# A bidirectional state space model beside attention: chunks of 16 tokens instead of 8, scans over four channel groups at once, and coefficients and softmax scaling moved off GpSimd

## The chip, the cores and the metric

One core of a Trainium2 chip runs the whole program. The metric is the device time of one execution in microseconds; the median of several executions counts. Engines are named as in the profile: PE (TensorE), DVE (VectorE), ACT (ScalarE), POOL (GpSimd), SP (which issues the DMAs).

## The reference

One encoder layer over 2048 tokens of width 1024, in float32. A projection gives q, k, v and a state space input u of 512 channels (32 groups of 16). Windowed attention and the state space model run on the same tokens; their outputs are joined, projected and followed by a feed-forward part.

```python
h  = rms_norm(x, norm1)
z  = h @ w_in                        # q (8 heads) | k, v (2 heads) | u (512)
a  = windowed_gqa(q, k, v, q_gain, k_gain, sink)
# s5_mixer, for each group g (16 channels) and both directions, 64 complex states:
abr, abi = mag * cos(li * dt), mag * sin(li * dt)
bur, bui = u_g @ bbr.T, u_g @ bbi.T
x_t = (abr + i abi) * x_{t-1} + (bur + i bui)_t
y   = d_skip * u + sum_dir( xr @ c_re.T - xi @ c_im.T )
s   = glu(gelu(y) @ w_glu)
x   = x + concat([a, s]) @ w_out
x   = x + square(relu(rms_norm(x, norm2) @ w_ff1)) @ w_ff2
```

## The kernel before, in words

**Stages.** From 0 to 132 us x is normalised and transposed and u is computed (`u_part`); beside that, `ssm_setup` makes the small tables of the state space model on DVE. From 132 to 362 us `qkv_part` makes q, k and v, tile by tile of 128 tokens. From 362 to about 790 us the attention runs, in 32 units (a block of 128 queries, and one of two key heads): `front` has scores and `softmax`, `back` the transposes of the probabilities, their product with v and the output projection. Then come the GLU, the second norm and the two feed-forward products, which the change does not touch.

**The side stream.** The state space model itself has no stage of its own: it is a Python generator, `side_stream`, that the qkv and attention loops advance. `Side.step(cost)` adds `cost * SIDE_STEPS / SIDE_MAIN` to a counter and takes that many steps of the generator; a `yield` in its functions ends a step. After the last group the stream loads w_glu and prepares the first quarter of the GLU. The recording layer then places each engine's instructions by an estimate of its own, so that an engine's queue is near the written order, but not the same; every engine works its queue strictly in order.

**The model in chunks.** Tokens are cut into chunks of T = 8, so 256 chunks. The states of both directions lie on the 128 partitions: 0 to 63 forward, 64 to 127 backward. For two groups at a time (16 pairs):
- `ssm_gen` makes coefficients: v (chunk input to state, on DVE, 6 instructions of 128x256), the rotation tables `t_c`, `t_s` (on POOL, 6 of 128x512) and q (state to chunk output, on POOL, 6 of 128x288); it copies `bb` into the `f` tiles (DVE) and loads u.
- `ssm_lag` transposes v on PE, makes the kernel of a chunk (`pkd`), stores it to DRAM (`kd_dr`) and loads it again as a Toeplitz matrix `tt`.
- `ssm_vu` multiplies: `pvu` = v by u, 128x256, copied to `b_r`, `b_i` by ACT.
- `ssm_scan` turns `b` into a rotating frame (L682, 6 instructions of 128x512), so that the recurrence over chunks is real, with one factor `rmag` per state; eight scans of 64x255 follow (real and imaginary part, two groups, two directions; L699, L701), and 6 more instructions turn the states back.
- `ssm_y` adds up `py` = tt by u + q by states, three products of 128x256 per group, and stores y.

**Softmax.** For four heads of a unit, DVE makes the negative maxima `nm` (L1002) and `es`; ACT takes four exponentials (L1007) and one for the sink; DVE adds up `den` and takes the reciprocal `rc` (L1012); POOL multiplies the four tiles p by `rc` (L1014).

Of the kernel before, what the change touches and what calls it, by code (L numbers as in the profile page):

```python
# [54 lines left out]
def hymba_kernel(ctx: ExitStack, tc: tile.TileContext, x, norm1, w_in, q_gain, k_gain, sink,  # L55
# [75 lines left out]
    KEEP, SCRATCH = 928, 2048  # L131

    def ssm_setup(scr):
# [178 lines left out]
        tt(mag, si[:, 0, :], MUL, o=pri[:, 1, :])
        for lo, n in ((1, 1), (2, 2), (4, 4)):
            br_ = prr[:, lo:lo + 1, :].to_broadcast([P, n, NG])
            bi_ = pri[:, lo:lo + 1, :].to_broadcast([P, n, NG])
            cmul(prr[:, 1:1 + n, :], pri[:, 1:1 + n, :], br_, bi_,
                 prr[:, lo + 1:lo + 1 + n, :], pri[:, lo + 1:lo + 1 + n, :])
# [1210 lines left out]
```

## Time and profile before

| | us |
|---|---|
| median of 3 runs | 2297.1 (2296.23 to 2302.04) |
| profiled execution, its own time | 2302.7 |
| its span, first to last instruction | 2300.5 |
| stretch of the projections with side work | 132 to 362 |
| stretch of the attention with side work | 362 to 735 |

Over the whole span PE is busy 2097.2 us (91%), DVE 1568.7 (68%), ACT 957.3 (42%), POOL 901.4 (39%). Busy time says nothing of which engine the others wait for, and an average over the span hides the stages; the stretches above are therefore looked at apart. Matmuls are pipelined, so that a busy PE can still have room.

### The profile page before, as it was taken

The numbers are of one execution on the slowest core, as the hardware profiler recorded it, in microseconds if no ns is written. First come the engines' busy times: TensorE is split into PE (matmuls) and PEld (weight loads), VectorE is DVE, ScalarE is ACT, GpSimd is POOL, SyncE is SP. The second block draws the span as 40 slices with busy tenths as digits, with TensorE's granted clock in tenths as the row PEclk, the third lists the DMA queues.
The fourth block names the chain that finished last, engine by engine and source line by source line (L and its number), as shares of the span: only waits on it lengthen the run. The fifth ranks groups of instructions, "written<-read, shape, count | busy, mean of one in ns | idle before, by whom it ended". The sixth has DMA issues, their size and how long they took to land.

```text
span 2300.5 us, 29626 instructions
## 1 busy us (share of the span) xinstructions
PE 2097.2 (91%) x10034; PEld 1705.8 (74%) x10034; DVE 1568.7 (68%) x2849; ACT 957.3 (42%) x1869; POOL 901.4 (39%) x768
## 2 busy tenths in 40 slices
PE   7988795788799999869999999999689999999999
PEld 7977674566566778658888788888577787788787
DVE  7869996898977564465555565555577767776765
ACT  5422123444445643245555665555423322332331
POOL 2043433566663422322222222222346535653541
PEclk9999997898989999979999999999899999999999
DMA  9824433222223544774444554443374433433334
GB/s 259 273 86 123 124 107 98 73 66 90 79 89 97 173 138 165 246 234 154 154 154 152 196 183 153 152 153 131 140 275 128 129 107 120 131 126 100 129 123 169
DMA packets 283895, 332.28 MB, mean 144 GB/s; under 512 B 62944, under 2 KB 210912, under 8 KB 283744
## 3 DMA queue, kind: packets, MB, share of 16 engines
q1 hardware_dynamic: 283744, 330.40, 43.9%
q8 instruction: 79, 1.29, 0.2%
q14 instruction: 72, 0.59, 0.1%
HBM read 201.91 MB, written 128.42 MB: 144 GB/s over the span
## 4 chain that ended last, share of the span: by engine, by line
PE 58%; DVE 25%; DMA 6%; POOL 4%; issue 4%; ACT 3%; SPq 1%; DVEq 0%; ACTq 0%; POOLq 0%
PE f L84 6%; PE f L85 6%; PE f L86 6%; PE f_al L86 5%; PE f_al L84 5%; PE f_al L85 5%; PE f_ga L86 2%; PE f_ga L85 2%; PE f_ga L84 2%; DVE t L682 2%; POOL w2s L1416 2%; DMA woraw<-in_w_out_dram 2%; DVE b_i L682 2%; POOL fs L1442 1%; DVE p L992 1%
## 5 line engine op out<-in xcount | busy, mean ns | idle before, releaser
L1487 DVE TENSOR_TENSOR acc<-f,acc 128x512 f32<-128x512 f32 x448 | 304.8, 687 | 164.8 <-PE f L86 159.7
L84 PE MATMUL f<-w2s,fs 128*128 128x512 f32 x896 | 352.8, 394 | 31.5 <-DVE acc L1487 15.6
L86 PE MATMUL f<-w2s,fs 128*128 128x512 f32 x896 | 351.2, 392 | 3.7 <-POOL fs L1442 3.7
L85 PE MATMUL f<-w2s,fs 128*128 128x512 f32 x896 | 351.1, 392 | 0.0
L1442 POOL TENSOR_TENSOR fs<-fr,fs 128x512 fp32r<-128x512 f32 x128 | 184.8, 1446 | 295.3 <-ACT fs L1441 247.3
L1441 ACT ACTIVATE fs<-fr 128x512 fp32r<-128x512 f32 x224 | 141.6, 633 | 364.9 <-PE f L86 341.3
L1285 POOL TENSOR_TENSOR w1s<-w1r,w1s 128x512 fp32r<-128x512 f32 x96 | 134.9, 1405 | 312.9 <-ACT w1s L1284 286.4
L84 PEld LDWEIGHTS f<-w2s,fs 128*128 128x128 f32 x896 | 169.4, 189 | 74.7 <-ACT fs L1441 26.2
L84 PE MATMUL f_al<-hb,w1s 128*128 128x512 f32 x512 | 201.0, 393 | 0.9 <-ACT w1s L1284 0.9
L86 PE MATMUL f_al<-hb,w1s 128*128 128x512 f32 x512 | 200.5, 392 | 1.2 <-DVE w1s L1285 1.1
L85 PE MATMUL f_al<-hb,w1s 128*128 128x512 f32 x512 | 200.3, 391 | 0.0
L86 PEld LDWEIGHTS f<-w2s,fs 128*128 128x128 f32 x896 | 169.6, 189 | 40.3 <-POOL fs L1442 4.5
L85 PEld LDWEIGHTS f<-w2s,fs 128*128 128x128 f32 x896 | 169.7, 189 | 34.5
L1014 POOL TENSOR_SCALAR p<-p,rc 128x384 f32<-128x384 f32 (+1 forms) x128 | 99.0, 790 | 121.1 <-DVE rc L1012 66.9
L1285 DVE TENSOR_TENSOR w1s<-w1c,w1s 128x512 fp32r<-128x512 f32 x96 | 67.2, 700 | 88.2 <-ACT w1s L1284 88.2
L86 PEld LDWEIGHTS f_al<-hb,w1s 128*128 128x128 f32 x512 | 96.5, 188 | 22.0 <-DVE w1s L1285 1.5
L84 PEld LDWEIGHTS f_al<-hb,w1s 128*128 128x128 f32 x512 | 96.5, 189 | 21.2 <-ACT w1s L1284 1.3
L85 PEld LDWEIGHTS f_al<-hb,w1s 128*128 128x128 f32 x512 | 96.6, 189 | 19.7
L1007 ACT ACTIVATE p<-p,nm 128x384 f32<-128x384 f32 (+1 forms) x128 | 75.4, 591 | 74.0 <-DVE nm L1002 74.0
L1284 ACT ACTIVATE w1s<-w1c 128x512 fp32r<-128x512 f32 x128 | 80.6, 630 | 50.6 <-PE f_al L86 48.4
L1416 POOL TENSOR_TENSOR w2s<-w2r,w2s 128x512 fp32r<-128x512 f32 x56 | 88.2, 1587 | 33.9 <-DMA w2r<-in_w_ff_dram 23.4
L85 PE MATMUL f_ga<-hb,w1s 128*128 128x512 f32 x256 | 99.9, 390 | 0.0
(525 smaller groups left out, 5250.4 us busy)
## 6 DMA issues: line engine op xcount, KB each, us to landing
fr<-f_dr SPq DMA_DIRECT2D x224, 256.0 KB
w1r<-in_w_ff_dram SPq DMA_DIRECT2D x64, 512.0 KB
f_dr<-fs SPq DMA_DIRECT2D x128, 256.0 KB
f_dr<-f SPq DMA_DIRECT2D x96, 256.0 KB
w2r<-in_w_ff_dram SPq DMA_DIRECT2D x32, 512.0 KB
hs<-hc_dr SPq DMA_DIRECT2D x56, 256.0 KB
xt<-in_x_dram SPq DMA_DIRECT2D x16, 512.0 KB
q_dr<-qd SPq DMA_DIRECT2D x16, 512.0 KB
```

What stands on the lines that cost most here:

```text
L84: nc.tensor.matmul(ps_ap, lhsT=lh, rhs=rh, start=first, stop=False, skip_group_check=onto)
L85: nc.tensor.matmul(ps_ap, lhsT=lh, rhs=rl, start=False, stop=False, skip_group_check=onto)
L86: nc.tensor.matmul(ps_ap, lhsT=ll, rhs=rh, start=False, stop=last, skip_group_check=onto)
L682: DVE.tensor_tensor(o, a, c, op=f)
L1007: ACT.activation(out=p[:, h, 0:w], in_=p[:, h, 0:w], func=AF.Exp, bias=nm[:, h:h + 1], accum_out=den[:, h:h + 1])
L1014: POOL.tensor_scalar(p[:, h, 0:w], p[:, h, 0:w], rc[:, h:h + 1], 0.0, op0=ALU.mult, op1=ALU.add)
L1284: ACT.activation(out=t[:, 0], in_=src, func=AF.Copy)
L1285: (DVE if m in (6, 7, 3) else POOL).tensor_tensor(t[:, 1], src, t[:, 0], op=SUB)
L1416: (DVE if m in (6, 7, 3) and fp else POOL).tensor_tensor(t[:, 1], src, t[:, 0], op=SUB)
L1441: ACT.activation(out=t[:, 0], in_=src, func=AF.Copy)
L1442: (DVE if m in (6, 7, 3) else POOL).tensor_tensor(t[:, 1], src, t[:, 0], op=SUB)
L1487: DVE.tensor_tensor(a[:, cs], po, a[:, cs], op=ADD)
```

## The change

It keeps the arithmetic of the model and regroups it.
- Chunks have C16 = 16 tokens, so there are NCH = 128 of them. Scans, rotations and tables take four groups at once (4 x 128 columns), in 8 rounds instead of 16 pairs. One scan runs through the four groups: its factor is now a tile `m` that holds zero at each group's end, and the source is set to zero there by four small memsets.
- Coefficients still come in pairs of groups: v and q are now 128x512 (16 tokens by 16 channels), with their tables stored so that the power index is contiguous. All of them, and the tables `t_c`, `t_s`, are made on DVE (`dv`). POOL has no part any more.
- The copies into the `f` tiles, the copy of `ks`, the tile `m` go to ACT.
- `pvu` and `py` take a chunk's two halves of 8 tokens in turn, with 128 columns each; the columns of u are reordered for that (`u_part`, and back in `glu`), and u comes in 16 loads of 64 columns per round.
- b, x, q, tt, ks and the tables have one buffer each; only u has two.
- Of the softmax multiplications by `rc` two of four go to DVE, two to ACT.
- The side stream's pacing: SIDE_STEPS 504 for 578, SIDE_MAIN 405 for 330, and in the projections each cost counts 1.6 times.

The bodies of the removed functions are in the listing above; of the setup only the table shapes are shown.

```diff
+C16 = 2 * T
+NCH = S // C16
...
-SIDE_STEPS = 16 * 34.0 + 14 + 20.0
-SIDE_MAIN = 330.0
+SIDE_STEPS = 8 * 61.0 + 16.0
+SIDE_MAIN = 405.0
+FIRST = 1.6
...
-    pw_r = sc.tile([P, T + 1, NG], F32, name="pw_r")
+    pw_r = sc.tile([P, NG, C16], F32, name="pw_r")
...
-                ACT.activation(out=uts[m][:, ::-1, o:o + 32], in_=pu.rearrange("p (c j) -> p j c", j=T), func=AF.Copy)
+                ACT.activation(out=uts[m][:, ::-1, o:o + 32].rearrange("p j (s c) -> p j s c", s=2),
+                               in_=pu.rearrange("p (c s j) -> p j s c", s=2, j=T), func=AF.Copy)
...
+    def dv(o, a, c, f):
+        DVE.tensor_tensor(o, a, c, op=f)
+
+    def ssm_load(i):
+        u = pm2.tile([P, 4, NC_], F32, tag="u", name="u")
+        for g in range(4):
+            for q in range(4):
+                src = u_dr[q, (4 * i + g) * GH:(4 * i + g + 1) * GH]
+                rows = bass.AP(src.tensor, src.offset, [[64, T], [T * 64, GH], [1, 64]])
+                nc.sync.dma_start(out=u[:, g, q * 64:(q + 1) * 64], in_=rows)
+        st[i] = {"u": u}
+
+    def ssm_tables(i):
+
+        gs = slice(4 * i, 4 * i + 4)
+        b = st[i]
+        m = pm.tile([P, 4, NCH], F32, tag="m", name="m")
+        for g in range(4):
+            ACT.activation(out=m[:, g, :], in_=ends, func=AF.Copy, scale=rmag[:, 4 * i + g:4 * i + g + 1])
+        b["m"] = m.rearrange("p g c -> p (g c)")
+        she = [P, 4, 8, 16]
+        tmp = pm.tile([P, 512], F32, tag="tmp", name="tmp")
+        te = tmp.rearrange("p (g a b) -> p g a b", g=4, a=8)
+        tc_, ts_ = (pm.tile(she, F32, tag=nm, name=nm) for nm in ("t_c", "t_s"))
+        ac, as_ = (four(a[:, gs], 3).to_broadcast(she) for a in (ta_c, ta_s))
+        bc, bs = (four(a[:, gs], 2).to_broadcast(she) for a in (tb_c, tb_s))
+        dv(tc_, ac, bc, MUL)
+        yield
+        dv(te, as_, bs, MUL)
+        yield
+        dv(tc_, tc_, te, SUB)
+        yield
+        dv(ts_, ac, bs, MUL)
+        yield
+        dv(te, as_, bc, MUL)
+        yield
+        dv(ts_, ts_, te, ADD)
+        b["t_c"], b["t_s"] = (a.rearrange("p g a b -> p (g a b)") for a in (tc_, ts_))
+        yield
+
+    def pair_in(i, h):
+
+        gs = slice(4 * i + 2 * h, 4 * i + 2 * h + 2)
+        b = st[i]
+        if h == 0:
+            for nm in ("b_r", "b_i"):
+                b[nm] = pm.tile([P, 4, NCH], F32, tag=nm, name=nm)
+        sh = [P, 2, C16, GH]
+        xr, xi = (four(a[:, gs], 2).to_broadcast(sh) for a in (bb_r, bb_i))
+        yr, yn = (four(a[:, gs], 3).to_broadcast(sh) for a in (pv_r, pv_n))
+        tmp = pm.tile([P, 512], F32, tag="tmp", name="tmp").rearrange("p (g s h) -> p g s h", g=2, s=C16)
+        v = {}
+        for j, (nm, x1, x2, op) in enumerate((("b_r", xr, xi, ADD), ("b_i", xi, xr, SUB))):
+            t = pm.tile(sh, F32, tag=f"v{j}", name="v")
+            dv(t, x1, yr, MUL)
+            yield
+            dv(tmp, x2, yn, MUL)
+            yield
+            dv(t, t, tmp, op)
+            yield
+            pt = ps.tile([P, 4, P], F32, tag="tr", name="ptv")
+            for q in range(4):
+                g, half = divmod(q, 2)
+                nc.tensor.transpose(pt[:, q, :], t[:, g, half * T:(half + 1) * T, :].rearrange("p s h -> p (s h)"),
+                                    ident)
+            vt = pm.tile([P, 4, P], F32, tag=f"vt{j}", name="vt")
+            ACT.copy(vt, pt)
+            v[nm] = vt
+        yield
+        for nm, vt in v.items():
+            pu = ps.tile([P, 2, NCH], F32, tag="ss", name="pvu")
+            for g in range(2):
+                us = b["u"][:, 2 * h + g, :].rearrange("p (b s c) -> p s b c", s=2, c=16)
+                for half in range(2):
+                    nc.tensor.matmul(pu[:, g, :], lhsT=vt[:, 2 * g + half, :], rhs=us[:, 1 - half],
+                                     start=half == 0, stop=half == 1)
+            ACT.copy(b[nm][:, 2 * h:2 * h + 2, :], pu)
+            yield
+
+    def ssm_rotate(i):
+        b = st[i]
+        br, bi = (b[nm].rearrange("p g c -> p (g c)") for nm in ("b_r", "b_i"))
+        tcs, tsn = b["t_c"], b["t_s"]
+        t1 = pm.tile([P, 4 * NCH], F32, tag="t1", name="t1")
+        t2 = pm.tile([P, 4 * NCH], F32, tag="tmp", name="tmp")
+        dv(t1, br, tcs, MUL)
+        yield
+        dv(t2, bi, tsn, MUL)
+        yield
+        dv(t1, t1, t2, ADD)
+        yield
+        dv(bi, bi, tcs, MUL)
+        yield
+        dv(br, br, tsn, MUL)
+        yield
+        dv(bi, bi, br, SUB)
+        for t in (t1, bi):
+            t3 = t.rearrange("p (g c) -> p g c", g=4)
+            DVE.memset(t3[FW, :, NCH - 1:NCH], 0.0)
+            DVE.memset(t3[BW, :, 0:1], 0.0)
+        b["s_r"], b["s_i"] = t1, bi
+        yield
+
+    def ssm_scan(i):
+
+        b = st[i]
+        n = 4 * NCH
+        m = b["m"]
+        for src, dst in ((b["s_r"], yr_t), (b["s_i"], yi_t)):
+            DVE.tensor_tensor_scan(dst[FW, 1:n], m[FW, 0:n - 1], src[FW, 0:n - 1], 0.0, op0=MUL, op1=ADD)
+            yield
+            yield
+            DVE.tensor_tensor_scan(dst[BW, n - 2::-1], m[BW, n - 1:0:-1], src[BW, n - 1:0:-1], 0.0,
+                                   op0=MUL, op1=ADD)
+            yield
+            yield
+
+    def ssm_unrotate(i):
+        b = st[i]
+        tcs, tsn = b["t_c"], b["t_s"]
+        xr, xi = (pm.tile([P, 4 * NCH], F32, tag=nm, name=nm) for nm in ("x_r", "x_i"))
+        t = pm.tile([P, 4 * NCH], F32, tag="tmp", name="tmp")
+        dv(xr, yr_t, tcs, MUL)
+        yield
+        dv(t, yi_t, tsn, MUL)
+        yield
+        dv(xr, xr, t, SUB)
+        yield
+        dv(xi, yi_t, tcs, MUL)
+        yield
+        dv(t, yr_t, tsn, MUL)
+        yield
+        dv(xi, xi, t, ADD)
+        b["x_r"], b["x_i"] = (a.rearrange("p (g c) -> p g c", g=4) for a in (xr, xi))
+        yield
+
+    def pair_out(i, h):
+
+        j = 2 * i + h
+        gs = slice(2 * j, 2 * j + 2)
+        b = {}
+        pr[i, h] = b
+        for nm, src in (("f_r", bb_r), ("f_i", bb_i)):
+            f = f_tiles[j % 2][nm]
+            ACT.copy(f[FW, :, 0, :], src[FW, gs])
+            ACT.copy(f[BW, :, 1, :], src[BW, gs])
+            b[nm] = f
+        sh = [P, 2, C16, GH]
+        cr, cn = (four(a[:, gs], 2).to_broadcast(sh) for a in (c_r, c_n))
+        er, ei = (four(a[:, gs], 3).to_broadcast(sh) for a in (pw_r, pw_i))
+        tmp = pm.tile([P, 512], F32, tag="tmp", name="tmp").rearrange("p (g s h) -> p g s h", g=2, s=C16)
+        for nm, x1, x2, op in (("q_r", cr, cn, ADD), ("q_n", cn, cr, SUB)):
+            t = pm.tile(sh, F32, tag=nm, name=nm)
+            dv(t, x1, er, MUL)
+            yield
+            dv(tmp, x2, ei, MUL)
+            yield
+            dv(t, t, tmp, op)
+            b[nm] = t
+            yield
+        pk = ps.tile([64, GH + C16 * GH], F32, tag="mm", name="pkd")
+        for n, (fn, qn) in enumerate((("f_r", "q_r"), ("f_i", "q_n"))):
+            for g in range(2):
+                nc.tensor.matmul(pk[g * 32:g * 32 + 32, GH:], lhsT=b[fn][:, g].rearrange("p d h -> p (d h)"),
+                                 rhs=b[qn][:, g].rearrange("p s h -> p (s h)"), start=n == 0, stop=n == 1)
+        for n, (bx, cx) in enumerate(((bb_r, c_r), (bb_i, c_n))):
+            for g in range(2):
+                nc.tensor.matmul(pk[g * 32:g * 32 + GH, 0:GH], lhsT=bx[:, 2 * j + g, :], rhs=cx[:, 2 * j + g, :],
+                                 start=n == 0, stop=n == 1)
+        ks = pm.tile([64, GH + C16 * GH], F32, tag="ks", name="ks")
+        ACT.copy(ks[:, GH:], pk[:, GH:])
+        for g in range(2):
+            o1 = slice(g * 32, g * 32 + GH)
+            DVE.scalar_tensor_tensor(ks[o1, 0:GH], dmask[o1, :], dcol[o1, j:j + 1], pk[o1, 0:GH], op0=MUL, op1=ADD)
+        for g in range(2):
+            nc.sync.dma_start(out=kd_dr[2 * j + g, :, C16 - 1:, :].rearrange("h m o -> h (m o)"),
+                              in_=ks[g * 32:g * 32 + GH, 0:C16 * GH])
+            nc.sync.dma_start(out=kd_dr[2 * j + g, :, 0:C16 - 1, :].rearrange("h m o -> h (m o)"),
+                              in_=ks[g * 32 + GH:g * 32 + 32, 2 * GH:])
+        yield
+        tt = pm.tile([P, 2, 3 * P], F32, tag="tt", name="tt")
+        for g in range(2):
+            src = kd_dr[2 * j + g]
+            win = bass.AP(src.tensor, src.offset, [[GH, T], [(2 * C16 - 1) * GH, GH], [1, 3 * P]])
+            nc.sync.dma_start(out=tt[:, g, :], in_=win)
+        b["tt"] = tt
+
+    def pair_y(i, h):
+        a, b = st[i], pr.pop((i, h))
+        py = ps.tile([P, 2, NC_], F32, tag="mm", name="py")
+        for g in range(2):
+            us = a["u"][:, 2 * h + g, :].rearrange("p (b s c) -> p s b c", s=2, c=16)
+            for half in range(2):
+                po = py[:, g, :].rearrange("p (q s c) -> p s q c", s=2, c=32)[:, half]
+                for si_ in range(2):
+                    w = 1 + half - si_
+                    nc.tensor.matmul(po, lhsT=b["tt"][:, g, w * P:(w + 1) * P], rhs=us[:, si_],
+                                     start=si_ == 0, stop=False)
+                for qn, xn in (("q_r", "x_r"), ("q_n", "x_i")):
+                    nc.tensor.matmul(po, lhsT=b[qn][:, g, half * T:(half + 1) * T, :].rearrange("p s h -> p (s h)"),
+                                     rhs=a[xn][:, 2 * h + g, :], start=False, stop=qn == "q_n")
+        ys = pm.tile([P, 2, NC_], F32, tag="ys", name="ys")
+        ACT.copy(ys, py)
+        for g in range(2):
+            c0 = (4 * i + 2 * h + g) * GH
+            nc.sync.dma_start(out=y_dr[c0:c0 + GH].rearrange("h j c -> j h c"), in_=ys[:, g, :])
+        yield
+
+    NB4 = NG // 4
+
+    def ssm_stream():
+        ssm_load(0)
+        yield from pair_in(0, 0)
+        yield from pair_in(0, 1)
+        yield from ssm_tables(0)
+        for i in range(NB4):
+            if i + 1 < NB4:
+                ssm_load(i + 1)
+            yield from ssm_rotate(i)
+            yield from pair_out(i, 0)
+            yield from ssm_scan(i)
+            yield from ssm_unrotate(i)
+            yield from pair_y(i, 0)
+            if i + 1 < NB4:
+                yield from pair_in(i + 1, 0)
+            yield from pair_out(i, 1)
+            if i + 1 < NB4:
+                yield from pair_in(i + 1, 1)
+                yield from ssm_tables(i + 1)
+            else:
+                for _ in range(8):
+                    yield
+            yield from pair_y(i, 1)
+            del st[i]
+...
-                    side.step(c)
+                    side.step(c * FIRST)
...
             for h in range(GQ):
-                POOL.tensor_scalar(p[:, h, 0:w], p[:, h, 0:w], rc[:, h:h + 1], 0.0, op0=ALU.mult, op1=ALU.add)
+                if h < 2:
+                    DVE.tensor_scalar(p[:, h, 0:w], p[:, h, 0:w], rc[:, h:h + 1], None, op0=ALU.mult)
+                else:
+                    ACT.activation(out=p[:, h, 0:w], in_=p[:, h, 0:w], func=AF.Copy, scale=rc[:, h:h + 1])
```

Where it moves instructions is seen in the engines' queues. First ACT, in the attention, around one unit's four exponentials (`p,den<-p,nm`) and the one of the sink (`es`). Before:

```order
L1025 COPY pT<-ptp 128x512 x2
L1007 ACTIVATE p,den<-p,nm 128x384 x4
L1009 ACTIVATE es<-es 128x4
L1025 COPY pT<-ptp 128x512
L977 ACTIVATE qs<-ptq 128x512
```

And now:

```order
L1040 ACTIVATE p,den<-p,nm 128x384 x4
L1042 ACTIVATE es<-es 128x4
L733 COPY ks<-pkd 64x256
L1061 COPY pT<-ptp 128x512
L1050 ACTIVATE p<-p,rc 128x384 x2
L1010 ACTIVATE qs<-ptq 128x512
L629 COPY vt<-ptv 128x512
L707 COPY f_r_1813<-bb_r 64x2x16
```

Two multiplications by the reciprocals `rc`, which DVE makes, now stand a few instructions behind the exponentials that they depend on, and side copies between them.

Second DVE, in the attention, from one unit's maxima or sums (`nm`, `den`) to its reciprocals. Before:

```order
L1002 SCALAR_TENSOR_TENSOR nm<-mx,nsink 128x4
L1058 TENSOR_TENSOR xr<-poa,xr 128x512
L1010 TENSOR_TENSOR den<-den,es 128x4
L1004 TENSOR_TENSOR es<-nm,nsink 128x4
L554 TENSOR_TENSOR v_r<-bb_r,pv_r 128x256
L1012 RECIPROCAL rc<-den 128x4
L562 TENSOR_TENSOR v_i<-bb_r,pv_n 128x256
```

And now:

```order
L564 TENSOR_TENSOR tmp<-bb_i,pv_n 128x512
L1025 ISA p,mx<-pss,dist 128x384
L1025 ISA mx 128x1
L1043 TENSOR_TENSOR den<-den,es 128x4
L564 TENSOR_TENSOR v<-v,tmp 128x512
L1045 RECIPROCAL rc<-den 128x4
L564 TENSOR_TENSOR t_s<-ta_c,tb_s 128x512
L1048 TENSOR_SCALAR p<-p,rc 128x384 x2
```

The side work between the links of the softmax is now of 128x512 throughout (`dv`, L564), with the tables among it, and the first two multiplications follow the reciprocal.

## Rows read from the trace of the kernel before

**Rows 1.** Windows of the three stretches; busy us (instructions) per engine, granted clock, DMA share, GB/s.
```profile
132.00:362.00 230.00, 190.46 (x1049) 161.87 (x1048) 214.26 (x433) 49.00 (x119) 103.84 (x99) 0.90 0.37 111
362.00:735.00 373.00, 299.67 (x1513) 218.59 (x1512) 306.56 (x711) 167.94 (x435) 201.34 (x217) 0.89 0.26 83
735.00:800.00 65.00, 62.66 (x294) 46.20 (x293) 37.78 (x72) 44.40 (x92) 28.65 (x28) 0.97 0.57 171
```

**Rows 2.** Chain of waits by line, first from 132 to 362, then from 362 to 735.
```profile
by line: DVE t L682 8.9%; DVE b_i L682 7.2%; DVE yr L701 5.1%; issue 5.1%; DVE b_r L682 5.0%; DVE yi L699 5.0%; DVE msq L888 4.6%; DVE yi L701 4.2%; DVE yr L699 3.8%; DVE sq L899 3.8%; DVE rsq L896 3.6%; DVE qd L905 3.5%; DVE msq L889 2.7%;
by line: DMA woraw<-in_w_out_dram 11.0%; DVE p L992 7.4%; DVE t L682 6.7%; DVE b_i L682 5.2%; ACT p L1007 4.8%; issue 4.5%; DVE yi L701 4.0%; DVE yr L701 3.9%; DVE b_r L682 3.8%; DVE yi L699 3.6%; DVE yr L699 3.6%; PE ptp L1023 3.4%; DVE xr
```

**Rows 3.** Windows, 132 to 735, VectorE: L682, L699, L701, tile tmpv, L554, L562, L610, L611.
```profile
132.00:735.00 603.00, 142.45 (x192) 0.89 0.30 93
132.00:735.00 603.00, 55.22 (x64) 0.89 0.30 93
132.00:735.00 603.00, 57.24 (x64) 0.89 0.30 93
132.00:735.00 603.00, 38.42 (x64) 0.89 0.30 93
132.00:735.00 603.00, 11.14 (x16) 0.89 0.30 93
132.00:735.00 603.00, 11.66 (x16) 0.89 0.30 93
132.00:735.00 603.00, 9.60 (x32) 0.89 0.30 93
132.00:735.00 603.00, 8.86 (x32) 0.89 0.30 93
```

**Rows 4.** One instruction of a tile or line: ns min/median/max, first and last start.
```profile
L701 DVE TENSOR_TENSOR_SCAN yr<-rmag,t x32: 685/1036/1391, 172.6 to 715.7; 64x255 f32<-64x255 f32 x32
L699 DVE TENSOR_TENSOR_SCAN yi<-rmag,b_i x32: 650/681/1387, 175.5 to 717.9; 64x255 f32<-64x255 f32 x32
L160 DVE TENSOR_TENSOR bb_r<-bb_r,scr x1: 694/694/694, 68.3 to 68.3; 128x512 f32<-128x512 f32 x1
L896 DVE TENSOR_TENSOR rsq<-rsq,t x16: 148/628/1111, 154.4 to 362.0; 128x10 f32<-128x10 f32 x16
L103 DVE TENSOR_SCALAR xt<-xt,rs x16: 752/753/755, 7.1 to 109.7; 128x1024 f32<-128x1024 f32 x16
L166 DVE TENSOR_SCALAR pw_r<-scr x3: 291/294/457, 1.0 to 58.8; 64x32 f32<-64x32 f32 x1, 64x288 f32<-64x288 f32 x1, 64x256 f32<-64x256 f32 x1
```

**Rows 5.** Groups of VectorE, 132 to 735: short instructions; busy us, mean ns, idle before.
```profile
L896 DVE TENSOR_TENSOR rsq<-rsq,t 128x10 f32<-128x10 f32 x16 | 9.1, 567 | 0.4
L894 DVE TENSOR_SCALAR t<-t 128x10 f32<-128x10 f32 x16 | 4.3, 270 | 0.2
L1002 DVE SCALAR_TENSOR_TENSOR nm<-mx,nsink 128x4 f32<-128x4 f32 x29 | 8.6, 295 | 0.1
L1010 DVE TENSOR_TENSOR den<-den,es 128x4 f32<-128x4 f32 x29 | 7.6, 262 | 12.0 <-ACT es L1009 11.9
```

**Rows 6.** Groups of ScalarE, 132 to 735.
```profile
L1007 ACT ACTIVATE p<-p,nm 128x384 f32<-128x384 f32 x108 | 65.1, 605 | 74.0 <-DVE nm L1002 74.0
L1009 ACT ACTIVATE es<-es 128x4 f32<-128x4 f32 x29 | 5.5, 190 | 0.0
```

**Rows 7.** Timeline of PE from 200: start us, duration us, instruction.
```profile
200.54 0.59 PE L718 MATMUL py<-u,tt 128*128 128x256 f32 x2
200.97 0.59 PE L719 MATMUL py<-b_r,q_r 128*128 128x256 f32 x2
```

**Rows 8.** Waits, 362 to 735: us in total, times, longest.
```profile
ACT p L1007 <- DVE nm L1002: 74.0, 19, 7.0
POOL p L1014 <- DVE rc L1012: 64.6, 8, 17.3
```

**Rows 9.** Issue of the loads of u on the DMA queue: ns min/median/max.
```profile
L617 SPq DMA_DIRECT2D u<-u_dr x32: 382/499/2807, 137.5 to 687.0; - x32
```

More of the change, by code (lines that the diff above doesn't have):

```diff
@@ L273, in ssm_setup @@
         yield
-        for ct, dst in zip(c_t, (c_r, c_i)):
+        for ct, dst, sg in zip(c_t, (c_r, c_n), (1.0, -1.0)):
             pt = ps.tile([P, 4, P], F32, tag="tr", name="ptc")
@@ L312, in ssm_setup @@
[L312 to L317, printed above, removed]
+        (prr, pvr), (pri, pvi) = ([a[:, o:o + C16 * NG].rearrange("p (s g) -> p s g", g=NG) for o in (3072, 3584)]
+                                  for a in (raw_l, raw_h))
@@ L318, in ssm_setup, with by_power @@
+        tt(mag, co[:, 0, :], MUL, o=prr[:, 0, :])
+        tt(mag, si[:, 0, :], MUL, o=pri[:, 0, :])
+        n = 1
+        while n < C16:
+            br_ = prr[:, n - 1:n, :].to_broadcast([P, n, NG])
+            bi_ = pri[:, n - 1:n, :].to_broadcast([P, n, NG])
+            cmul(prr[:, 0:n, :], pri[:, 0:n, :], br_, bi_, prr[:, n:2 * n, :], pri[:, n:2 * n, :])
+            n *= 2
             yield
+        def by_power(a):
+            return a.rearrange("p g s -> p s g")
         f, w = slice(0, NS), slice(NS, P)
-        for src, dst, sg in ((prr, pw_r, 1.0), (pri, pw_n, -1.0)):
-            ts(src[f], sg, MUL, o=dst[f])
-            ts(src[w, 0:1, :], sg, MUL, o=dst[w, 0:1, :])
-            ts(src[w, T:0:-1, :], sg, MUL, o=dst[w, 1:T + 1, :])
+        for src, dst in ((prr, pw_r), (pri, pw_i)):
+            ve.tensor_copy(by_power(dst)[f], src[f])
+            ve.tensor_copy(by_power(dst)[w], src[w, ::-1, :])
@@ L324, in ssm_setup @@
         yield
-        pvr, pvi = new([P, T, NG]), new([P, T, NG])
-        for src, dst in ((prr, pvr), (pri, pvi)):
-            ve.tensor_copy(dst[f], src[f, 0:T, :])
-            ve.tensor_copy(dst[w], src[w, T - 1::-1, :])
-        e8 = [a[:, 1:2, :].to_broadcast([P, T, NG]) for a in (co, si)]
-        cmul(pvr, pvi, e8[0], e8[1], pv_r, pv_n, conj=True)
+        for src, dst, one in ((prr, pvr, 1.0), (pri, pvi, 0.0)):
+            ve.memset(dst[f, 0, :], one)
+            ve.tensor_copy(dst[f, 1:C16, :], src[f, 0:C16 - 1, :])
+            ve.memset(dst[w, C16 - 1, :], one)
+            ve.tensor_copy(dst[w, 0:C16 - 1, :], src[w, C16 - 2::-1, :])
@@ L331, in ssm_setup @@
+        yield
+        e16 = [a[:, 1:2, :].to_broadcast([P, C16, NG]) for a in (co, si)]
+        cmul(pvr, pvi, e16[0], e16[1], by_power(pv_r), by_power(pv_n), conj=True)
         ts(pv_n, -1.0, MUL, o=pv_n)
@@ L342, in ssm_setup @@
         ve.reciprocal(rden, den)
-        am1 = ts(prr[:, 1, :], -1.0, ADD)
-        abi = pri[:, 1, :]
+        am1 = ts(prr[:, 0, :], -1.0, ADD)
+        abi = pri[:, 0, :]
         yield
@@ L366, in ssm_setup @@
             ec, es = co[:, j, :], si[:, j, :]
-            n = 1
-            while n < 16:
+            n, top = 1, tc_.shape[2]
+            while n < top:
                 ecb = ec.rearrange("p (g o) -> p g o", o=1).to_broadcast([P, NG, n])
@@ L535, in hymba_kernel @@
     for y in (yr_t, yi_t):
-        POOL.memset(y[0:NS, :, 0:1], 0.0)
-        POOL.memset(y[NS:P, :, NC_ - 1:NC_], 0.0)
-    st = {}
+        POOL.memset(y[0:NS, 0:1], 0.0)
+        POOL.memset(y[NS:P, 4 * NCH - 1:4 * NCH], 0.0)
+    POOL.memset(ends, 1.0)
+    POOL.memset(ends[0:NS, NCH - 1:NCH], 0.0)
+    POOL.memset(ends[NS:P, 0:1], 0.0)
+    MUL, ADD, SUB = ALU.mult, ALU.add, ALU.subtract
+    FW, BW = slice(0, NS), slice(NS, P)
+    st, pr = {}, {}
     def four(a, axis):
```

219 lines of the change are left out of this document (18 added, 201 removed).

## The prediction

> **What bounds the kernel now.** The change touches one part of the run, the stretch in which the state space model's side work runs beside the projections and the attention. I read the windows first, to see which engine fills that stretch. From 132 to 362 us (projections) VectorE is busy 214.3 of 230 us, 93%, and from 362 to 735 us (attention) 306.6 of 373, 82%; TensorE has 190.5 and 299.7, with a granted clock of 0.90 and 0.89, means over its two levels, 1.2 and 2.4 GHz [rows 1]. From 735 to 800 us, with the side work done, TensorE is busy 62.7 of 65 us at a clock of 0.97. So while the side work lasts, TensorE has holes and a lower clock. The chain of waits says who makes the holes: in the projections its longest entries are VectorE's rotations (L682) and scans (L699, L701), then VectorE's short normalising instructions (L888 to L896); in the attention the first entry is the load of w_out (11.0%), which is untouched, and then VectorE again, spread over scores, rotations and scans [rows 2]. VectorE is the bound in both, less purely in the second.
>
> The third reading is how long one VectorE instruction takes. A scan over 255 elements takes 650 ns at least and 681 in the median at one place, 1036 in the median at another; an addition over 10 elements takes 148 ns or 628 [rows 4]. The same work, up to four times as long: something holds it up. GpSimd, busy 103.8 and 201.3 us in these stretches [rows 1], is the candidate, since short instructions that do almost nothing are stretched as well.
>
> **The change, part by part.** The sum is made against the profiled execution: 2302.7 us, span 2300.5. The median shown is 2297.1, 5.6 less; a saving is taken from either alike.
>
> *VectorE, removed.* 192 rotations 142.5 us, 128 scans 55.2 + 57.2, the 96 instructions that make v 38.4 + 11.1 + 11.7, 64 copies into the f tiles 9.6 + 8.9 [rows 3]: 334.6 us.
>
> *VectorE, added.* Eight rounds of four groups have, each, 6 tables, 12 for v, 6 to rotate, 6 to turn back and 12 for q: 42 instructions of 128x512, 336 in all. The only one of today's that reads a coefficient repeated along its innermost axis took 694 ns [rows 4]: 336 x 0.69 = 232 us. 32 scans of 511: twice 0.681 is 1.36 us at most, less one fixed part of 0.15 (the shortest instruction there, [rows 4]) 1.21 at least; I take 1.21, since the row it comes from pays that part once per instruction, 39 us. 32 memsets at 0.15 or less: 5 us. 64 multiplications of p by 1/denominator: rows of the same form are 753 ns at 1024 elements and 291 at 256 to 288 (64 partitions), so between 0.29 and 0.75 and, by their slope, 0.36: 23 us. Together 299.
>
> *VectorE, relieved.* GpSimd no longer has an instruction between its first memsets and the loads of w_glu. The nine kinds of short instruction that stay (six of 16 from L896 to L894, three of 29, L1002, L1004, L1010) add up to 40 and 24 us; 183 at about 0.15 are 28 [rows 4, 5]: 36 saved. The rest of what stays is hardly stretched.
>
> VectorE's balance: 520.8 - 334.6 + 299 - 36 = 449, **72 us less work**. Nearly all of it is relief: with the stretched times taken out on both sides, the old side work and the new are about the same size.
>
> *TensorE, added.* The output product of two groups was 12 records of 256 columns and becomes 32 of 128; a record pair of 256 starts 0.43 us after the one before it [rows 7], 0.215 each. By columns, 128 take half, 0.107: 3.4 us per two groups instead of 2.6. The transposes double (4 more, at most 0.22 each), the kernel-table product doubles its columns (0.9 more at most). Some 2.4 us x 16 = 38 us of 490. The bounds of a half-width record are 0.107 and 0.215 (as dear as the full width, because a weight load or the new output pattern sets the pace); I take 0.107, since the cost in the rows follows the columns.
>
> On that pattern the Trainium skill ("PSUM — Partial Sum Buffer", Specifications) speaks against the change: it says that a matmul writing PSUM in a non-contiguous pattern is slowed significantly, and the new product writes runs of 32 floats with gaps of 32. No matmul of this trace writes that way, so no run here shows it; by that rule the upper bound, 0.215, would hold or be passed.
>
> *ScalarE, added.* 64 multiplications of p at 0.6 (L1007's size), 64 f copies at 0.19 [rows 6], 16 more evacuations at 0.6, tables m and ks: some 70 us on 217 of 603. The idle half of ScalarE covers that; if it does not, the transposed p (L1025) comes late.
>
> *Queues.* SP issues 128 small loads of u in place of 32, at 0.5 us each [rows 9] 48 us more in 603; a round's loads go out a round before their use, and that hides them. The order shows stores of q and the reloads of h behind them, with tens of us of slack. GpSimd loses work that VectorE or ScalarE now do. The setup in the first 132 us changes by a few instructions under TensorE's cover: nothing. The new u layout costs nothing either: as many elements per instruction.
>
> *From work to time.* The side stream's pacing (step count over main cost, and the new factor 1.6) moves its share inside the projections from 219 of 578 steps (38%) to 249 of 504 (49%). Projections: VectorE loses 127 of the 334.6 and 26 of the relief and gains 136: about 197 instead of 214. At 93% that would be 212 us, but TensorE there gains about 29 us on 190.5, so it is as full as VectorE: I take 222, **8 saved**. Attention: VectorE 251 instead of 306.6. If VectorE set everything at 82%, 306 us, 67 saved; if TensorE's own busy time plus 10 us set it, nothing. TensorE's 299.7 hold slow-clock time that comes back as the waits go, so I lean to the first: 334, **39 saved**. Sum 47: 2302.7 - 47 = 2255.7 here, 2250 against the median.
>
> **The rivals.**
>
> *VectorE stays the bound in both stretches.* Then 18 + 67 = 85 come out: 2212. For it: rows 2. Against: TensorE is nearly full in the projections afterwards.
>
> *Half-width products cost as much as full ones.* 32 records at 0.215 instead of 0.107 in the output product and 16 in the state product are 5.1 us x 16 = 83 us more on TensorE; at the rate of this forecast (47 of 72) some 54 us: 2302.7 - 47 + 54, in medians about 2300, no difference. For it: nothing in the trace has this form. Against: [rows 7].
>
> *The stretching was not GpSimd's.* Then the relief of 36 is gone, 336 instructions cost 0.74 (142.5 over 192, [rows 3]) and 32 scans 0.88 of the old kind twice over: 36 + 17 + 17 of the 72 go, and about 2295 is left. Against it: no other user of VectorE's data sits in that stretch.
>
> *Single buffers make VectorE and TensorE wait in turn: slower.* q, v, tt, ks, b and the tables now have one buffer, where q, tt, ks, b and the tables had two. In the order, VectorE's first q of the next two groups waits for TensorE's output product of the last two, and that product stands in TensorE's queue behind attention work which itself waits for VectorE's maxima. There are 16 such places; all else on VectorE stands behind. At 3 us each (48 us) the saving is eaten; at 5 us, 80 lost against 47: 2330. For it: ScalarE already waits 74.0 us for VectorE's maxima and GpSimd 64.6 us, up to 17.3 at once, for reciprocals [rows 8], so queues run that far behind. Against: some 9 steps (5 us of side work) lie between product and next q.
>
> **How the numbers follow.** Forecast 0.60 (its own range 2228 to 2275); VectorE alone 0.18; half-width dear 0.08; GpSimd innocent 0.06; slower 0.08. A difference under 0.3%, 7 us, cannot be told from none here. Faster: 0.60 + 0.18 and a little of the two null cases, 0.79; same 0.12; slower 0.09. The range reaches down past 2212 by the unknown prices (scan, p) to 2205, and up over the two null cases to 2298.
>
> **What would show it.** Right: GpSimd idle until the loads of w_glu; scans of 511 near 1.2 us with minimum and median together; additions over 10 elements near 0.15; VectorE near 450 us in the stretch; the granted clock above 0.90; the end of the projections some 8 us and of the attention some 47 us earlier; the same lengths after that. Wrong: new instructions of 128x512 well over 0.69; output products 0.215 apart; VectorE idle in front of q behind TensorE; ScalarE as the first entry of the chain in the attention; or a stretch that ends with w_glu's loads exposed.

## The result, and the profile after

The changed kernel takes 2230.7 us (median of 4 runs, 2224.0 to 2234.6) against 2299.4 of the kernel before (4 runs): a ratio of 0.9699 with an interval of 0.9670 to 0.9728, 69 us or 3.0% saved. The profiled execution took 2234.64 us, its span 2232.9.

Where it came from, by windows of the kernel after that end with the last projection and with the last output product of the state space model:

```profile
134.00:345.00 211.00, 198.73 (x1325) 171.78 (x1324) 184.14 (x428) 69.89 (x197) 1.12 (x11) 0.98 0.45 136
345.00:672.00 327.00, 286.50 (x1797) 220.81 (x1795) 249.55 (x700) 212.59 (x568) 0.00 (x0) 0.94 0.32 99
```

and the same two stretches of the kernel before, cut the same way:

```profile
134.00:348.00 214.00, 181.50 (x993) 154.41 (x992) 201.52 (x401) 45.91 (x110) 96.36 (x93) 0.91 0.38 114
348.00:730.00 382.00, 301.63 (x1532) 221.28 (x1530) 317.22 (x736) 167.64 (x437) 206.55 (x219) 0.88 0.25 81
```

VectorE (third busy column) falls from 518.7 to 433.7 us, ScalarE rises from 213.6 to 282.5, GpSimd is idle. TensorE issues 265 more products in the attention and yet is busy 15 us less there: its granted clock is 0.94 instead of 0.88 (shares of full speed).

The first and the last score product of each kernel, before and after, by tile (first and last start stand behind the durations):

```profile
L990 PE MATMUL pss<-k_hh,qs x128: 278/422/690, 367.0 to 753.0; 128*128 128x384 f32 x112, 128*128 128x256 f32 x16
```

```profile
L1023 PE MATMUL pss<-k_hh,qs x128: 274/339/689, 357.4 to 680.7; 128*128 128x384 f32 x112, 128*128 128x256 f32 x16
```

The attention starts 9.6 us earlier and ends 72 earlier. Later stages keep their lengths: the last addition of the attention's output starts 70 us earlier, and 68 are left at the end of the profiled execution. So some 10 us were saved in the projections and some 60 in the attention.

The chain of waits of the kernel after in the attention, 345 to 672, by line (it answers to the second line of [rows 2]):

```profile
by line: DMA woraw<-in_w_out_dram 9.3%; PE pv L1069 8.1%; PE ptp L1059 7.0%; PE pss L1023 5.0%; PE poa L88 4.7%; PE poa L87 4.6%; PE poa L89 4.6%; PE pss L1024 4.1%; PE pvu L637 4.0%; DVE p L1025 3.7%; PE ptq L1008 3.4%; ACT p L1040 2.9%; P
```

Before, VectorE's rotations and scans filled this list behind the load of w_out; now TensorE's products do. VectorE's groups, 134 to 692, answer to [rows 4, 5]:

```profile
L929 DVE TENSOR_TENSOR rsq<-rsq,t 128x10 f32<-128x10 f32 x16 | 2.7, 167 | 0.3
L1035 DVE SCALAR_TENSOR_TENSOR nm<-mx,nsink 128x4 f32<-128x4 f32 x32 | 5.2, 162 | 0.8 <-ACT p L1040 0.6
L1048 DVE TENSOR_SCALAR p<-p,rc 128x384 f32<-128x384 f32 (+1 forms) x62 | 22.7, 408 | 0.3
L564 DVE TENSOR_TENSOR q_r<-c_r,pw_r 128x512 f32<-128x512 f32 x16 | 10.9, 683 | 18.5 <-PE py L762 18.5
L672 DVE TENSOR_TENSOR_SCAN yr<-m,t 64x511 f32<-64x511 f32 x8 | 9.7, 1210 | 0.0
L675 DVE TENSOR_TENSOR_SCAN yi<-m,b_i 64x511 f32<-64x511 f32 x8 | 9.8, 1220 | 0.2
```

The short instruction over 10 elements (`rsq<-rsq,t`, a multiplication, though the prediction and the expectations call it an addition), 567 ns in the mean before, takes 167. Among the waits, ScalarE's for the maxima have gone from 74.0 us [rows 8] to 11.3:

```profile
DVE q_r L564 <- PE py L762: 18.5, 4, 10.5
DVE p L1025 <- PE pss L1024: 16.9, 15, 2.5
ACT p L1040 <- DVE nm L1035: 11.3, 8, 5.5
```

### The profile page after: what moved, and what is told of

The parts are those of the page before. It is cut to its first block, busy times and chain, and to the rows that moved or that the text cites. A ratio compares the mean times of both kernels' runs of the same rounds, so it can differ in the third digit from the quotient of the medians.

```text
span 2232.9 us, 30461 instructions
## 1 busy us (share of the span) xinstructions
PE 2084.3 (93%) x10546; PEld 1710.8 (77%) x10546; DVE 1478.7 (66%) x2806; ACT 1016.1 (46%) x2061; POOL 591.5 (26%) x451
## 4 chain that ended last, share of the span: by engine, by line
PE 63%; DVE 15%; DMA 8%; POOL 5%; issue 4%; ACT 3%; SPq 2%; DVEq 0%; POOLq 0%; ACTq 0%
PE f L87 6%; PE f L89 6%; PE f L88 6%; PE f_al L87 5%; PE f_al L89 5%; PE f_al L88 5%; POOL w2s L1452 3%; PE f_ga L89 2%; PE f_ga L87 2%; PE f_ga L88 2%; POOL fs L1478 1%; PE pv L1069 1%; DMA woraw<-in_w_out_dram 1%; DVE acc L1523 1%; PE f_be L88 1%
## 5 line engine op out<-in xcount | busy, mean ns | idle before, releaser
L818 POOL TENSOR_TENSOR wgl<-wgr,wgh 128x512 fp32r<-128x512 f32 x8 | 10.4, 1317 | 555.2 <-DMA wgr<-in_w_glu_dram 542.4
L88 PE MATMUL f_ga<-hb,w1s 128*128 128x512 f32 x256 | 99.9, 390 | 0.0
L87 PE MATMUL f_ga<-hb,w1s 128*128 128x512 f32 x256 | 99.8, 390 | 0.0
L89 PE MATMUL f_ga<-hb,w1s 128*128 128x512 f32 x256 | 99.7, 389 | 0.0
```

The lines of the kernel that those rows point to most:

```text
L87: nc.tensor.matmul(ps_ap, lhsT=lh, rhs=rh, start=first, stop=False, skip_group_check=onto)
L88: nc.tensor.matmul(ps_ap, lhsT=lh, rhs=rl, start=False, stop=False, skip_group_check=onto)
L89: nc.tensor.matmul(ps_ap, lhsT=ll, rhs=rh, start=False, stop=last, skip_group_check=onto)
L818: eng_lo.tensor_tensor(lo, raw, hi, op=ALU.subtract)
```

## The experiments

Ratios are against the kernel before on the same chip. To compare: the change has 0.9699 (0.9670 to 0.9728).

### Is it GpSimd? Idle work put beside the changed kernel

`last` holds the tile m of the round that runs; nobody reads `junk`.

```diff
+    junk = pm.tile([P, 4 * NCH], F32, name="junk")
     def dv(o, a, c, f):
         DVE.tensor_tensor(o, a, c, op=f)
+        if last:
+            POOL.tensor_tensor(junk, last["m"], last["m"], op=MUL)
```

> The changed kernel with 276 multiplications of 128x512 on GpSimd beside it whose result nobody reads (the scratch tile and these instructions are all that is added). Theory S: VectorE's additions over 10 elements go back from 0.167 to over 0.35 us in the mean, scans of 511 from 1.21 to 1.5 or more, VectorE's total in the stretch rises by 60 to 90 us, and the time goes to 2280 to 2310. Rival R (the regrouping into larger instructions gave the time, GpSimd is of no matter): VectorE's instructions keep their lengths, 2222 to 2240.

2386.5 us, ratio 1.0384 (1.0365 to 1.0402): 156 us lost, more than the whole saving. From 134 to 830:

```profile
L936 DVE TENSOR_TENSOR rsq<-rsq,t 128x10 f32<-128x10 f32 x16 | 10.4, 648 | 0.3
L567 DVE TENSOR_TENSOR t<-b_r,t_c 128x512 f32<-128x512 f32 x8 | 7.1, 894 | 1.8 <-ACT b_r L646 1.8
```

```profile
L569 POOL TENSOR_TENSOR junk<-m 128x512 f32<-128x512 f32 x276 | 360.3, 1305 | 235.6 <-ACT m L586 214.6
```

The stretching is GpSimd's. The expectation had the direction and not the size: VectorE is busy 172 us longer (169 of them are length beyond that of undisturbed instructions of the same line and form), where 60 to 90 were expected, and 2280 to 2310 was passed by 76 us. The scans met a multiplication only 4 times in 32, so their part of the expectation failed. Splitting VectorE's 128x512 instructions by whether a GpSimd one ran beside over half of each: 1398 ns in the median with it (206 of them), 685 without (172). It works both ways: a multiplication on GpSimd takes 1.04 us where no two-tensor instruction of VectorE lies beside it, and 1.37 in the median where one does. Reductions (806 to 813 ns) and reciprocals do not change.

The second run replaces the multiplication by a memset that reads nothing (ScalarE writes the tile once per round to release them):

```diff
-            POOL.tensor_tensor(junk, last["m"], last["m"], op=MUL)
+            POOL.memset(junk, 0.0)
```

> As the run with GpSimd's idle multiplications, but with 276 memsets of 128x512 in their place: GpSimd writes the same tile and reads nothing. Theory S2 (VectorE waits for a GpSimd instruction that reads as VectorE reads): VectorE's instructions keep their lengths, additions over 10 elements stay near 0.167, 2222 to 2240. Rival (any GpSimd instruction holds VectorE up): additions over 10 elements above 0.3 and 2280 or more.

2224.8 us, ratio 0.9690 (0.9673 to 0.9706): nothing lost. All of GpSimd's 145 us lie in the projections (139 to 306 us), so the attention had no memset beside it. The last projection product starts at 343.7 us (in the changed kernel at 345.2, beside multiplications at 439.5).

```profile
L569 POOL MEMSET junk<- 128x512 f32 x276 | 145.2, 526 | 23.0 <-ACT junk L607 7.6
L937 DVE TENSOR_TENSOR rsq<-rsq,t 128x10 f32<-128x10 f32 x16 | 2.7, 167 | 0.3
L935 DVE TENSOR_SCALAR t<-t 128x10 f32<-128x10 f32 x16 | 4.9, 308 | 0.0
```

VectorE's instructions with two tensors keep their lengths: 167 ns over 10 elements, and 683 over 512 with a memset beside over half of each (137 of them), 685 without. An instruction with one tensor and numbers (L935, 163 ns in the changed kernel) goes to 308. It is the kind of GpSimd instruction that counts, not its busy time. The Trainium skill ("SBUF — State Buffer", Who interferes with whom) says just this: a VectorE instruction with two SBUF inputs contends with a GpSimd one that reads SBUF and not with one that only writes, and forms like tensor_scalar can, in a mode that takes both port pairs, contend with either; whoever comes second waits until the other's instruction ends. These two runs agree, by the lengths above.

### Which part: the softmax, the coefficients, or the regrouping?

The softmax scaling alone, in the kernel before, and put back on GpSimd in the changed one (the reverse edit):

```diff
-                POOL.tensor_scalar(p[:, h, 0:w], ... rc[:, h:h + 1], 0.0, op0=ALU.mult, op1=ALU.add)
+                if h < 2:
+                    DVE.tensor_scalar(p[:, h, 0:w], ... rc[:, h:h + 1], None, op0=ALU.mult)
+                else:
+                    ACT.activation(out=p[:, h, 0:w], ... func=AF.Copy, scale=rc[:, h:h + 1])
```

> The kernel before with one part of the change alone: two of four softmax multiplications on VectorE, two on ScalarE, none on GpSimd. Theory S (GpSimd's instructions slow VectorE's, and the time follows VectorE): VectorE takes on 64 multiplications (24 us) and is relieved of the stretching that goes with 92 of GpSimd's 305 us, some 20 to 25 us, so the balance is near zero: 2285 to 2305. Rival P (the shorter softmax chain is what the attention gained): 2260 or less, with ScalarE's wait for the maxima well under 74 us.

> The changed kernel with all four softmax multiplications back on GpSimd, the rest as changed. Theory S: VectorE loses 24 us and gets some 20 us of stretching back, ScalarE loses 34 us: 2220 to 2245. Rival P (the softmax chain): 2260 or more.

Alone: 2304.2 us, 1.0024 (1.0012 to 1.0037). Put back: 2228.1, 0.9702 (0.9675 to 0.9729). So this part gives nothing in either kernel. The number of the first held, its reason did not: the time by which VectorE's instructions are longer than the median undisturbed one of their line and form, about 92 us in the kernel before, only fell to 90 (7 of them on the new multiplications), since GpSimd's coefficient work stayed. That is 0.42 us for each of the 215 us of two-tensor work left on GpSimd, beside 0.47 in the run with idle multiplications. Put back, 94 us of scaling lengthen VectorE's instructions by only some 10:

```profile
L1047 POOL TENSOR_SCALAR p<-p,rc 128x384 f32<-128x384 f32 (+1 forms) x128 | 94.4, 755 | 442.3 <-DMA woraw<-in_w_out_dram 230.5 <-DVE rc L1045 48.2 <-ACT pT L1058 39.3
```

It isn't that nothing is held up. VectorE's short instructions `es` over 4 elements last up to 527 ns, to the end of the scaling (some 160 alone), and of 72 instructions of 128x512 that meet a scaling, 28 last over 800 ns. But 308 others never meet one, and GpSimd's instructions are lengthened as well: 586 ns alone, 1010 in the median beside a two-tensor instruction of VectorE.

GpSimd's coefficients with the new grouping (`gp` is the same instruction on GpSimd), and VectorE's with the old one (tables, q and scaling moved, chunks of 8 kept):

```diff
-        dv(tc_, ac, bc, MUL)
+        gp(tc_, ac, bc, MUL)
...
-            dv(t, x1, er, MUL)
+            gp(t, x1, er, MUL)
```

> The changed kernel with its 48 table and 96 q instructions on GpSimd (with a scratch tile of its own), the softmax as changed. VectorE loses 144 x 0.685 = 99 us. Theory S2 (VectorE waits out a GpSimd instruction of two inputs: 169 us for 276 of them in the run with GpSimd's idle multiplications, 0.61 each) gives 88 back, a balance of -11: 2215 to 2240. Rival X (work moved off the engine that bounds is a gain): 2150 to 2175. Rival Y (GpSimd now makes q too late for TensorE): 2260 or more.

```diff
-        POOL.tensor_tensor(b["t_c"], ac, bc, op=ALU.mult)
+        DVE.tensor_tensor(b["t_c"], ac, bc, op=ALU.mult)
...
-        yield from cprod(POOL, b["q_r"], b["q_n"], ...
+        yield from cprod(DVE, b["q_r"], b["q_n"], ...
```

> The kernel before with tables and q on VectorE and the softmax multiplications split, so GpSimd is idle, but with chunks of 8 and two groups at a time. VectorE gains 96 x 0.69 + 96 x 0.4 to 0.6 + 24 = 128 to 148 us and loses the 93 us by which its instructions are longer than undisturbed ones of their form in the trace of before: +35 to +55. Theory S2 with the regrouping as the saving: 2325 to 2355. Rival I (the idle GpSimd alone gives the gain): 2245 or less.

With the scaling split the same way in all four, they make a table:

| | coefficients on GpSimd | on VectorE |
|---|---|---|
| chunks of 8, two groups | 2304.2, 1.0024 (1.0012 to 1.0037) | 2266.2, 0.9867 (0.9850 to 0.9883) |
| chunks of 16, four groups | 2288.9, 0.9961 (0.9947 to 0.9975) | 2230.7, 0.9699 (0.9670 to 0.9728) |

Neither half makes the result alone: by the medians the regrouping gives 15 us beside a busy GpSimd and 36 beside an idle one, the move 38 and 58. Theory S2 missed both numbers: with the coefficients back on GpSimd the time came out in the range of rival Y (2260 or more), and chunks of 8 on VectorE fell between the two ranges. Chunks of 8 on VectorE alone were to be slower and are 31 us faster; windows that end with the last projection and the last output product:

```profile
134.00:320.60 186.60, 172.70 (x997) 146.89 (x996) 180.31 (x460) 46.44 (x111) 0.73 (x8) 0.98 0.44 131
320.60:704.00 383.40, 307.77 (x1567) 220.35 (x1565) 347.09 (x934) 198.94 (x499) 0.00 (x0) 0.89 0.25 81
```

VectorE is busy 527.4 us against 518.7 before, 9 more where 35 to 55 were expected. I had added recorded lengths, and these overlap. From 134 us to the end of the attention the recorded lengths of VectorE's instructions do add up to 38 us more (656 against 618), as expected, and the overlaps take back 31. In the changed kernel, on VectorE:

```profile
442.32 0.68 DVE L564 TENSOR_TENSOR q_r<-c_r,pw_r 128x512 f32<-128x512 f32 x1
442.92 0.68 DVE L564 TENSOR_TENSOR q_n<-c_n,pw_r 128x512 f32<-128x512 f32 x1
443.52 0.68 DVE L564 TENSOR_TENSOR q_r<-q_r,tmp 128x512 f32<-128x512 f32 x1
```

An instruction lasts 0.68 us by its record, but the next starts after 0.60. The Trainium skill ("Perfetto Trace Analysis", Optimizing Scalar/DVE Operations) says that half of the overhead in a recorded latency overlaps with the next instruction; here it is 0.08 us, beside some 0.06 on that page. So the gain is not less work on VectorE but less idle time, 43 us of these windows instead of 77.

The tables put back on GpSimd, cut the same way:

```profile
134.00:375.00 241.00, 206.10 (x1322) 177.41 (x1321) 193.71 (x356) 70.19 (x196) 103.35 (x86) 0.95 0.39 119
375.00:729.00 354.00, 294.98 (x1800) 227.46 (x1799) 244.31 (x629) 213.08 (x569) 94.73 (x70) 0.92 0.28 91
```

VectorE's total, 438.0, is near that of the changed kernel (433.7), as expected (its instructions are 81 us longer than undisturbed ones, for 88), and still 58 us are lost: it is idle 157 us instead of 104. The timeline shows why one of its instructions is late (the short normalising ones, with GpSimd beside them):

```profile
257.65 0.30 DVE L925 TENSOR_SCALAR msq<-msq 128x10 f32<-128x10 f32 x1
258.00 1.26 POOL L576 TENSOR_TENSOR q_n<-q_n,tmpq 128x512 f32<-128x512 f32 x1
258.48 0.81 DVE L928 TENSOR_TENSOR t<-rsq 128x10 f32<-128x10 f32 x1
259.34 1.07 POOL L576 TENSOR_TENSOR tmpq<-ta_s,tb_s 128x512 f32<-128x512 f32 x1
259.40 1.03 DVE L931 TENSOR_TENSOR rsq<-rsq,hsc 128x10 f32<-128x10 f32 x1
260.49 1.29 POOL L576 TENSOR_TENSOR t_c<-t_c,tmpq 128x512 f32<-128x512 f32 x1
260.55 1.25 DVE L932 TENSOR_TENSOR rsq<-rsq,t 128x10 f32<-128x10 f32 x1
```

Each two-tensor instruction over 10 elements that starts within a GpSimd instruction ends with it (10 in this run, each 22 to 26 ns after it). These stand in a chain to the results that TensorE works on next, so a microsecond here can delay TensorE, which 99 us of work taken off VectorE elsewhere do not repair. Rival Y, the longer way from q over tt to the output product (six GpSimd instructions of 1.2 to 1.5 us in place of 0.60), shows little in the list of waits: TensorE waits 13.8 us for q and tt against 8.4 in the changed kernel, but 36.6 against 16.6 for VectorE's other results and 47.4 against 31.4 for ScalarE's. What of these a late q causes in turn was not separated.

### Pacing, pattern, buffers

> The changed kernel with the side stream paced as before: no factor 1.6 in the projections, main cost 330. Theory S: the same VectorE work, only more of it in the attention; the projections end some 5 to 10 us earlier and the attention later, 2222 to 2245 in all. Rival Q (the new pacing is what filled the projections and gave the time): 2260 or more.

```diff
-SIDE_MAIN = 405.0
-FIRST = 1.6
+SIDE_MAIN = 330.0
+FIRST = 1.0
```

2232.7 us, 0.9716 (0.9700 to 0.9732). The total is as expected, the shift is not: the projections end 23 us earlier instead of 5 to 10, and the last score product starts at 678.3 instead of 680.7, no later. So the pacing moves work and saves none.

> The changed kernel with the output product written in plain runs of 128 columns; ScalarE's evacuation puts the columns in order instead (two copies of 256 columns in place of one of 512). Theory C (the cost of a record follows its columns, not the pattern of its output): records 0.107 to 0.112 us apart as in the changed kernel, 2223 to 2238. Rival D (the patterned output slows a product): records well closer together than 0.111 and 2220 or less.

```diff
-                po = py[:, g, :].rearrange("p (q s c) -> p s q c", s=2, c=32)[:, half]
+                po = py[:, g, half * NCH:(half + 1) * NCH]
```

2228.2 us, 0.9701 (0.9687 to 0.9716): no difference. The output products of the changed kernel, in their pattern, and of this run, in plain runs:

```profile
508.28 0.39 PE L762 MATMUL py<-x_r,q_r 128*128 128x128 f32 x2
508.50 0.39 PE L762 MATMUL py<-x_i,q_n 128*128 128x128 f32 x2
```

```profile
508.08 0.39 PE L762 MATMUL py<-x_r,q_r 128*128 128x128 f32 x2
508.30 0.39 PE L762 MATMUL py<-x_i,q_n 128*128 128x128 f32 x2
```

Pairs start 0.22 us apart in both.

> The changed kernel with two buffers for q_r and q_n instead of one (to make room, the tile m is written from one column, in 64 ScalarE instructions in place of 32). If the single buffer costs what the waits show: VectorE's 18.5 us in front of q_r are gone and the time falls by 5 to 15: 2216 to 2226. If the wait lies beside other waits: 2226 to 2236. The rival of the prediction (single buffers make both engines wait in turn): under 2200.

```diff
-            t = pm.tile(sh, F32, tag=nm, name=nm)
+            t = pm2.tile(sh, F32, tag=nm, name=nm)
```

2223.8 us, 0.9688 (0.9671 to 0.9705). The wait in front of q is gone from the list. The time lies in the first range, 7 us below the changed kernel's by the medians, but the intervals overlap, so it is not to be told from it.

### What bounds the changed kernel

> The changed kernel, in which the rotation tables of the first four groups serve all (the other 28 groups get wrong tables; 42 VectorE instructions, 29 us, are left out). If VectorE still sets the pace: 2200 to 2212. If TensorE or a chain between engines does: 2220 to 2235.

```diff
+        if i > 0:
+            for nm in ("t_c", "t_s"):
+                b[nm] = st0[nm]
...
+            return
```

> The changed kernel without the second score product (q by the low part of k, 128 products of 384 columns; the scores lose precision, VectorE still makes the low part). TensorE loses 128 x 0.17 = 22 us of 287 in the attention. If TensorE sets the pace there now: 2204 to 2214. If VectorE does, or waits that don't move with TensorE's work: 2222 to 2235. (29 us off VectorE gave 9.)

```diff
-            nc.tensor.matmul(pss, lhsT=qs[:, h, :], rhs=k_ll[:, g, ks], start=False, stop=True)
```

29 us less on VectorE by recorded lengths (23 by windows): 2221.9, 0.9677 (0.9657 to 0.9696), 5 by the ratios and not to be told from none. 22 us less on TensorE: 2213.4, 0.9638 (0.9622 to 0.9654), 14 by the ratios, with the intervals apart. So the attention's pace follows TensorE's work more than VectorE's after the change. The product left out also stands in front of VectorE's scores, whose wait for it falls from 16.9 to 10.6 us; whether TensorE's throughput or that link pays was not separated.

> The changed kernel with the eight loads of w_out issued in the first attention unit instead of the second to fourth; the splitting stays where it was. The loads are 8.8% of the chain in the attention after the change, some 30 us, with up to 15 us from issue to landing. If they are late because they are issued late: 10 to 25 us less, 2205 to 2220. If the transfer itself or ScalarE's queue is what takes the time: 2224 to 2236.

```diff
+                if u == 0:
+                    for a in wo_parts[2 * h:2 * h + 2]:
+                        fetch_wo(*a)
```

2235.2 us, 0.9741 (0.9724 to 0.9758): no gain, in the second range, and ScalarE still waits 26.2 us for these loads (22.6 in the changed kernel). But the edit brought them forward by little. Their issue in the changed kernel and in this run:

```profile
L989 SPq DMA_DIRECT2D woraw<-in_w_out_dram x8: 503/1106/5562, 361.1 to 395.2; - x8
```

```profile
L989 SPq DMA_DIRECT2D woraw<-in_w_out_dram x8: 524/3789/7399, 358.6 to 390.7; - x8
```

Seven now stand in a row, and issuing these alone takes 26.8 us, up to 7.4 for one; each load starts 2 to 11 us earlier. So what a much earlier load would give stays open. Of the runs that keep the whole result, none is told apart from the changed kernel as faster.

## Why the prediction was right, and where it was short

The measured 2230.7 us lie at the lower edge of the forecast's own range (2228 to 2275), as far from its 2250 as from the 2212 of the rival in which VectorE stays the bound.

**The bound and its cause** were right: VectorE held up by GpSimd. The short kinds named were 35 us longer than undisturbed ones of their form, where 36 were forecast, and now those of 10 elements are at 0.16 to 0.17 each. Scans of 511 take 1.21 to 1.22 as taken, ScalarE's scaling 0.61 for 0.6, ScalarE's added work 69 us for "some 70"; VectorE's scaling 0.41 for 0.36. The half-width record starts 0.11 after the one before it, the lower bound. So the rival of dear half-width products is out, and with it the rule of the Trainium skill ("PSUM — Partial Sum Buffer", Specifications) for this pattern: plain runs were no faster.

**VectorE's added work was mis-sized.** 336 x 0.69 = 232 us used recorded lengths; by starts they cost 0.60 each, 202. The balance "72 us less" was 85 by the windows above. The removed rotations are overcounted in the same way, only fewer of them.

**The projections**: 8 forecast, 9.6 measured to the first score product. The number held, its terms less well: the last projection product starts only 2.8 us earlier, the rest lies between it and the attention, and TensorE was busy 198.7 us where 219.5 were forecast, at a granted clock of 0.98 instead of 0.91.

**The attention** holds the step that was wrong: "if TensorE's own busy time plus 10 us set it, nothing", and from there a value between, 334. By its own figures this bound is not nothing: 299.7 plus 10 is 310 of 373 us, 63 saved. Both bounds then lie at 63 to 67, and from the first to the last score product 62.7 came (386.0 to 323.3 us). With 63 for the 39, the sum gives 2232 for the profiled execution, which took 2234.6. Nor were TensorE's busy us a fixed amount, since they held slow-clock time, as the text said: the granted clock rose from 0.88 to 0.94, and 1797 products took 286.5 us where 1532 had taken 301.6. That the time stayed within the range owes something to the range's width.

The rival in which VectorE stays the bound (2212) did not come either: with VectorE's work gone, a cut in TensorE's work pays more than one in VectorE's, as the runs with one set of tables and with one score product show.

**The rival of single buffers** has its place in the trace (18.5 us in front of q, 4 waits) and no price that the runs can tell: a second buffer for q changes the time by less than the intervals. The other single buffers were not tried. **The rival that the stretching is not GpSimd's** is out by the runs with idle multiplications and memsets.

**What the sum missed** is that work and time part. It priced the move of the coefficients as work that VectorE gains against relief it gets. The table shows that moving them pays 38 to 58 us, while VectorE's busy time in the two runs with chunks of 16 is nearly equal (438 and 434 us).

## What to carry to other kernels

Before giving GpSimd work beside a busy VectorE, ask what both read. A short two-tensor instruction of VectorE that starts within a GpSimd instruction that reads two tensors waits it out, and if it stands in a chain for TensorE, the loss can be larger than VectorE's busy time shows. Idle memsets cost nothing here, idle multiplications 156 us. Price back-to-back instructions by their starts, not their recorded lengths, and do not take the busy time of a TensorE at a low granted clock as fixed. When a bound is set by an engine's busy time, subtract it from the stretch before calling the saving nothing.

## What was not expected of the hardware

GpSimd's one-tensor scaling held VectorE up by some 10 us for 94, where its two-tensor instructions cost 169 us for 360, and GpSimd's instructions are themselves lengthened beside VectorE's (586 to 1010 ns and 1.04 to 1.37 us in the median). And a kernel with more VectorE work (527 for 519 us busy) was 31 us faster, with GpSimd idle and none of VectorE's instructions lengthened by it.
